# Seven of twelve weave distances changed in a two-layer gated trunk on one TensorE-bound core

## The chip, the core and the metric

The kernel runs on one core of a Trainium2 chip. The metric is the device time of one execution in microseconds. Before the change it was 1135.04 us, the median of three runs that lay between 1132.31 and 1135.21 us.

## What is computed

Two layers over a residual stream x of 512 positions by 1024 features, float32. Each layer normalises, scales and shifts x by a conditioning vector, makes one wide projection, runs three causal token mixers beside each other and merges them through gates.

```python
u = rms_norm(x, norm_g) * (1 + scale[:, None]) + shift[:, None]
z = u @ w_in     # aq ak av ag iq ik iw | bq bk bv bg | cq ck cv cg | ma mb mc
# A: indexer scores -> the 128 best keys of each query -> softmax attention, 8 heads, rotary
# B: sliding window of 128, 8 query heads on 2 key heads, learned sinks, rotary
# C: stick-breaking attention, 8 heads, strictly causal
merged = (sigmoid(ma) * (ya @ w_br_a) + sigmoid(mb) * (yb @ w_br_b) + sigmoid(mc) * (yc @ w_br_c))
return x + gate[:, None] * (merged @ w_out)      # ya, yb, yc already times silu(ag), silu(bg), silu(cg)
```

## The kernel before, in words

Everything is held transposed: features on the 128 partitions, the 512 positions along the free axis. A float32 product is made of three matmuls of a rounded type: the weight chunk is split into a high part `whi` and a low part `wlo`, the activation into `uh` and `ul` (or the two halves of `Y` for a mixer's output), and the products high-high, high-low and low-high are added. One column tile of the projection (`ttile`, 128 columns, for example aq2 or mb1) is two halves of 12 matmuls, and one output tile of a branch (`branch_item`, for example tile 1 of branch b) is 12 matmuls; such a group of 12 is called a block here. Each block needs one weight chunk of 128x512 that SyncE's queue (SP) loads into `wstage` and that VectorE, ScalarE or GpSimd split.

A mixer handles two heads at a time, four pairs p = 0 to 3, in three stages. Its score stage (`c_qk`, `softmax_qk`) multiplies `Q` by `KH` into five PSUM banks of the pool `ps_s` (four for B), adds the low products (`klow`), then VectorE adds the mask and takes the maximum (for A the mask is `score`, which must first have been through the top-k loop), ScalarE makes the exponentials and their sum, and VectorE or ScalarE scale them into the tile `X`. Its transpose stage (`softmax_tr32`) transposes `X` on VectorE in four pieces and moves 16 blocks of it by DMA into `U` (pairs 0 and 2) or into a part of `V5` (`V_675` in the order's rows; pairs 1 and 3); ScalarE's queue and SP share these issues. Its value stage (`value_run`, in `pairs`) multiplies `U` or `V` by the values on TensorE. Pair a0's value product rides along with the score stage of a1 (`RIDE`); a1 and a2 have theirs together, behind all of branch b; a3 has its own.

The order of the work comes about in two steps. First a weave (`Weave.run`) writes one list from seven streams: the three mixers, the indexer, the top-k loop, the conditioning products of this and the next layer, and the stream of projection and branch tiles. A stream that yields `wait(n)` is left out until n nanoseconds of planned TensorE work have been written. The distances are in the table `SPACE`: for mixer a, `a0` stands before a pair's score stage, `a1` between its scores and its transposes, `a2` between these and its value product; b and c likewise; `ag` and `as` space the conditioning products of this and the next layer, `t` the top-k steps.

```python
            yield need(f"ak{p}" if b == "a" else f"bq{p}")
            yield wait(SPACE[b + "0"])
            ...
            yield softmax_qk(b, p)
            ...
            yield wait(SPACE[b + "1"])
            yield softmax_tr(b, p)
            yield put(f"{b}free{p}")
            yield wait(SPACE[b + "2"])
```

Second, a recorder (`Recorder`) takes this list, gives buffers out in its order, and plans every instruction onto the engines by costs of its own and by how late each may go; it may move instructions past each other, and it chooses between VectorE, ScalarE and GpSimd for splits and copies. The programs of the five engines are then fixed: at run time each engine goes through its own list in order. All instructions come from two lines, L621 and, for `pairs`, L619.

Of the kernel before, what the change touches and what calls it, by code (L numbers as in the profile page):

```python
# [39 lines left out]
TOPK = 128  # L40
WARM = 8
BIG = 2.0 ** 100
SPACE = {"c0": 865, "c1": 7720, "c2": 1802, "a0": 1361, "a1": 13022, "a2": 500, "b0": 2448, "b1": 10119, "b2": 1676, "ag": 12129, "as": 6930, "t": 2422}
QCOST = 2408
BKEY = "cfree2"
LOAD_AHEAD, SPLIT_AHEAD = 4, 3
# [585 lines left out]
def op(cost, fn, *chunks):  # L632
    return ("op", cost, fn, [c + (phase[0],) for c in chunks])


def wait(ns):
    return ("wait", ns)


def need(e):  # L640
    return ("need", e)


def put(e):
    return ("set", e)
# [3 lines left out]
def trunk(ctx, tc, xT, vecs, w_ss, w_gt, w_first, w_t, w_v, w_br, w_o, rope, consts, out):  # L649
# [498 lines left out]
    def topk():  # L1148
        yield need("idx")
        for i in (1, 2, 3):  # L1150
            for n in range(TOPK // 8):
# [5 lines left out]
                yield op(0, fn)  # L1157
                yield wait(SPACE["t"])

# [81 lines left out]
    def mixer_c():  # L1241
        for p in range(4):
            yield need(f"ck{p}")
            yield wait(SPACE["c0"])
            yield from riders("c", p, RIDE.get(("c", p), ()), "in")
            yield c_qk(p)
            yield from riders("c", p, RIDE.get(("c", p), ()), "out")
            yield wait(SPACE["c1"])
            yield softmax_tr("c", p)
            yield put(f"cfree{p}")  # L1250
            yield wait(SPACE["c2"])
            for g in GROUPS["c"]:
# [131 lines left out]
    def softmax_tr(b, p):  # L1384
        if p in TR32.get(b, ()):
            return softmax_tr32(b, p)

        def fn():
            pt = st.pop(("p", p))
            pos, tpos = (bpos, btpos) if b == "b" else (apos, cpos)  # L1390
            nb = 4 if b == "b" else 5
            tb, PT, left = [None] * nb, [None] * nb, [0] * nb
            for e in range(2):
                for j in range(4):
                    left[tpos(e, j)[0]] += 1
            for e in range(2):
                for j in range(4):
                    bk, c0 = tpos(e, j)
                    if tb[bk] is None:
                        tb[bk] = sbank()  # L1400
                    for i in (range(j, min(4, j + 2)) if b == "b" else range(j, 4)):
                        sbk, s0 = pos(e, i)
                        kc = s0 + 128 * j - keys(b, i)[0]
                        PE.transpose(tb[bk][:, c0 + 128 * (i - j):c0 + 128 * (i - j) + 128], pt[sbk][:, kc:kc + 128], ident)
                    left[bk] -= 1
                    if not left[bk]:
                        W = 384 if b == "b" and bk >= 2 else 512
                        if all(v is None for v in PT):
                            whole = st["V5"] if b != "c" and p % 2 else rec.tile("U", [P, 5 * S], F32)
                        PT[bk] = whole[:, S * bk:S * bk + S]  # L1410
                        cast(PT[bk][:, :W], tb[bk][:, :W])
            st["pt", p] = PT
        return op(1520 if b == "b" else 2180, fn)
# [33 lines left out]
    def riders(b, p, ps, stage):  # L1447
        for q in ps:
            if stage == "out":
                yield put(f"{b}pv{q}")  # L1450
                continue
            yield need(f"{b}g{q}")
            if q and b != "c":
                yield need("brc" if b == "b" else "brb")

    def mixer_ab(b):
# [3 lines left out]
        for p in range(4):  # L1460
            yield need(f"ak{p}" if b == "a" else f"bq{p}")
            yield wait(SPACE[b + "0"])
            yield from riders(b, p, RIDE.get((b, p), ()), "in")
            yield softmax_qk(b, p)
            yield from riders(b, p, RIDE.get((b, p), ()), "out")
            yield wait(SPACE[b + "1"])
            yield softmax_tr(b, p)
# [348 lines left out]
```

## Time and profile before

| what | value |
|---|---|
| runs, us | 1132.31, 1135.04, 1135.21 |
| profiled execution, us | 1133.6 |
| its span from the first to the last instruction, us | 1131.7 |
| TensorE matmul busy | 1113.8 us, 98% |
| VectorE, ScalarE, GpSimd busy | 921.6, 607.0, 237.5 us |
| granted TensorE clock, mean | 0.999 |
| HBM read, written | 125.39 MB, 4.19 MB |

The names in the profile are those of the program without buffer numbers: `m<-zs` is the shift by half a head that the rotary step needs (its tile is m2), `U<-X` and `V<-X` are the DMAs of the transpose stage. An engine's row shows in brackets how long it stood idle before and what ended that. A matmul of 512 columns shows 0.39 us in its row, but the next one starts about 0.23 us after it; so TensorE can lose time between two starts without an idle time being shown.

### The profile page before, as it was taken

To read this page: it belongs to the slowest core of one execution; us is meant where nothing else is said; L and a number is where in the kernel's file an instruction comes from. 1 tells how busy PE (TensorE), PEld (TensorE's weight loads), DVE (VectorE), ACT (ScalarE), POOL (GpSimd) and SP (SyncE) were. 2 spreads that over 40 slices of the span, in tenths; PEclk is the share of its full clock that TensorE was granted. 3 is DMA by queue.
4 is the path that set the end of the run, shared out by engine and by line. 5 is a ranking of instruction groups with operands and counts; after the bars stand their busy time and mean duration, and the time that the engine had idled before them with its cause. 6 is when DMAs were issued, how large, how long until landed. Compare 5 with 4: busy or idle time off the path is not lost.

```text
span 1131.7 us, 17615 instructions
## 1 busy us (share of the span) xinstructions
PE 1113.8 (98%) x5539; PEld 922.8 (82%) x5539; DVE 921.6 (81%) x2016; ACT 607.0 (54%) x1285; POOL 237.5 (21%) x307
## 2 busy tenths in 40 slices
PE   8999999999999899999999999999999999999997
PEld 6899877788887687788898987777888788877886
DVE  8855999999999897787585479999999898666654
ACT  6744767663555553444355357685546366443343
POOL 1200344512223211010001004452212232111101
PEclk9999999999999999999999999999999999999999
DMA  9744343555465575455533443435635445525343
GB/s 358 233 122 123 98 118 105 147 163 146 116 182 159 148 213 160 140 149 180 179 114 103 110 131 85 132 102 163 182 103 144 135 141 151 150 82 149 94 131 102
DMA packets 95837, 162.48 MB, mean 144 GB/s; under 512 B 15104, under 2 KB 29696, under 8 KB 95744
## 3 DMA queue, kind: packets, MB, share of 16 engines
q1 hardware_dynamic: 86720, 147.44, 44.4%
q10 hardware_dynamic: 9024, 13.92, 4.3%
q8 instruction: 44, 0.72, 0.3%
q14 instruction: 49, 0.40, 0.1%
HBM read 125.39 MB, written 4.19 MB: 115 GB/s over the span
## 4 chain that ended last, share of the span: by engine, by line
PE 77%; DVE 15%; DMA 4%; SPq 1%; ACT 1%; issue 1%; POOL 0%; DVEq 0%; ACTq 0%; POOLq 0%
PE ps_z L621 60%; PE ps_s L621 14%; DVE t L621 4%; PE ps_s L619 2%; DVE X L621 1%; SPq L621 1%; DVE wlo L621 1%; DMA m<-zs 1%; PE ps_z L619 1%; DVE score L621 1%; DVE m L621 1%; DMA U<-X 1%; DVE zc L621 1%; DVE e L621 1%; DMA Y<-in_w_ss 1%
## 5 line engine op out<-in xcount | busy, mean ns | idle before, releaser
L621 PE MATMUL ps_z<-uh,whi 128*128 128x512 f32 (+1 forms) x905 | 352.9, 391 | 0.4 <-DVE G L621 0.3
L621 PE MATMUL ps_z<-ul,whi 128*128 128x512 f32 (+1 forms) x905 | 352.0, 390 | 0.2 <-DVE ul L621 0.2
L621 PE MATMUL ps_z<-uh,wlo 128*128 128x512 f32 (+1 forms) x905 | 350.3, 388 | 0.0
L621 DVE TENSOR_TENSOR wlo<-wstage,whi 128x512 fp32r<-128x512 f32 (+2 forms) x294 | 193.2, 661 | 99.2 <-ACT whi L621 90.0
L621 ACT CAST whi<-wstage 128x512 fp32r<-128x512 f32 (+2 forms) x226 | 133.7, 593 | 234.2 <-PE ps_z L621 176.2
L621 PEld LDWEIGHTS ps_z<-uh,whi 128*128 128x128 f32 x905 | 169.7, 188 | 36.7 <-issue 1.2
L621 PEld LDWEIGHTS ps_z<-ul,whi 128*128 128x128 f32 x905 | 169.9, 188 | 34.2 <-issue 1.2
L621 PEld LDWEIGHTS ps_z<-uh,wlo 128*128 128x128 f32 x905 | 169.9, 188 | 34.1
L621 POOL TENSOR_TENSOR wlo<-wstage,whi 128x512 fp32r<-128x512 f32 (+2 forms) x78 | 99.7, 1279 | 230.5 <-DVE whi L621 116.5
L621 PE MATMUL ps_z<-Y,whi 128*128 128x512 f32 x384 | 119.2, 391 | 0.2
L621 POOL CAST whi<-wstage 128x512 fp32r<-128x512 f32 (+1 forms) x72 | 43.6, 606 | 318.4 <-PE ps_z L621 177.6
L621 PEld LDWEIGHTS ps_z<-Y,whi 128*128 128x128 f32 x384 | 71.8, 188 | 16.7 <-DVE Y L621 1.1
L621 ACT ACTIVATE e<-e 128x512 f32<-128x512 f32 x96 | 59.9, 629 | 39.3 <-DVE e L621 30.9
L621 ACT ACTIVATE t<-t,nm 128x256 f32<-128x256 f32 (+3 forms) x128 | 65.2, 511 | 24.2 <-DVE nm L621 15.4
L621 PE MATMUL ps_z<-Y,wlo 128*128 128x512 f32 x192 | 74.4, 389 | 0.0
L621 ACT ACTIVATE t<-t 128x512 f32<-128x512 f32 x100 | 56.1, 627 | 0.3
L621 DVE STREAM_TRANSPOSE X<-X 128x640 f32<-128x640 f32 (+1 forms) x80 | 55.9, 738 | 0.4 <-ACT X L621 0.2
L621 DVE MAX8 m<-score 128x8 f32<-128x256 f32 (+2 forms) x96 | 53.4, 556 | 1.3
L621 ACT ACTIVATE e<-ps_z 128x512 f32<-128x512 f32 x68 | 40.3, 593 | 22.1 <-DVE wlo L621 5.2
L621 DVE MATCH_REPLACE8 score<-m,score 128x256 f32<-128x256 f32 (+2 forms) x96 | 52.0, 542 | 0.0
L621 PE MATMUL ps_s<-KH,Q 128*128 128x256 f32 (+3 forms) x280 | 49.7, 305 | 1.3 <-DVE e L621 0.7
L621 PEld LDWEIGHTS ps_s<-KH,Q 128*128 128x128 f32 x280 | 42.0, 189 | 8.8 <-DVE e L621 1.6
(211 smaller groups left out, 1953.5 us busy)
## 6 DMA issues: line engine op xcount, KB each, us to landing
wstage<-in_w_t SPq DMA_DIRECT2D x212, 256.0 KB, 2.7
wstage<-in_w_v SPq DMA_DIRECT2D x48, 182.0 KB, 2.3
m<-zs SPq DMA_DIRECT2D x128, 64.0 KB, 2.0
wstage<-in_w_gt SPq DMA_DIRECT2D x32, 256.0 KB, 2.7
wstage<-in_w_ss SPq DMA_DIRECT2D x32, 256.0 KB, 2.9
wstage<-in_w_o SPq DMA_DIRECT2D x32, 256.0 KB, 2.7
Y<-in_w_ss SPq DMA_DIRECT2D x15, 512.0 KB, 5.9
U<-X SPq DMA_DIRECT2D x65, 80.0 KB, 2.7
```

The lines of the kernel that those rows point to most:

```text
L619: self.real[engine].matmul(*[real(a) for a in q[:3]], start=q[3], stop=True, skip_group_check=True)
L621: made = getattr(self.real[engine], y.op)(*[real(a) for a in y.args], **{k: real(v) for k, v in y.kw.items()})
```

## The change

The table gets new distances; nothing else differs.

```diff
-SPACE = {"c0": 865, "c1": 7720, "c2": 1802, "a0": 1361, "a1": 13022, "a2": 500, "b0": 2448, "b1": 10119, "b2": 1676, "ag": 12129, "as": 6930, "t": 2422}
+SPACE = {"c0": 1375, "c1": 7720, "c2": 1666, "a0": 1325, "a1": 18965, "a2": 500, "b0": 2568, "b1": 9198, "b2": 1676, "ag": 12129, "as": 6748, "t": 2422}
```

The programs have the same 5319 rows on TensorE before and after, of which some stand elsewhere. On the others a handful of splits and copies change engine: VectorE has 1841 rows before and 1837 after, ScalarE 1331 and 1340, GpSimd 312 and 307. On TensorE the order is the same up to the end of mixer c, apart from two matmuls of tile mc2 that now stand between the first and the second matmuls of branch c; it differs from b's last pair to a's last pair, and is the same again from there on. The same holds in layer 2.

**TensorE, layer 1, the scores of pair a2.** Rows `uh`/`ul` are blocks of the projection, `KH,Q` the scores, `klow,Q` their low products. Before, they stand in pieces between the matmuls of tiles mb1 and aq3:

```order
L621 MATMUL ps_z<-ul_253,whi 128x512
L621 MATMUL ps_s<-KH,Q 128x512 x2
L621 MATMUL ps_z<-uh_425,wlo 128x512
L621 MATMUL ps_s<-KH,Q 128x384
L621 MATMUL ps_s<-KH,Q 128x128
L621 MATMUL ps_z<-uh_472,whi 128x512
L621 MATMUL ps_z<-ul_494,whi 128x512
L621 MATMUL ps_z<-uh_472,wlo 128x512
L621 MATMUL ps_s<-KH,Q 128x384
L621 MATMUL ps_s<-KH,Q 128x128
L621 MATMUL ps_s<-KH,Q 128x256 x2
L619 MATMUL ps_s<-klow_80,Q 128x512 x2
```

After, they stand together between the two halves of aq3:

```order
L621 MATMUL ps_z<-uh_384,wlo 128x512
L621 MATMUL ps_s<-KH,Q 128x512 x2
L621 MATMUL ps_s<-KH,Q 128x384 x2
L621 MATMUL ps_s<-KH,Q 128x128 x2
L621 MATMUL ps_s<-KH,Q 128x256 x2
L621 MATMUL ps_s<-klow_80,Q 128x256
L619 MATMUL ps_s<-klow_80,Q 128x512 x2
L619 MATMUL ps_s<-klow_80,Q 128x384 x2
```

The same happens to the scores of a0, a1 and a3. With it the distances between them change. In layer 1 the order has, from the last score row of a0 to the first of a1, 4 blocks before and 10 after; from the last of the main group of a1 to the first of a2, 5 blocks and some matmuls before and 10 after; from the last of a2 to the value product of a1 and a2, 21 blocks before and 13 after. From the scores of b3 to the value product of b2 and b3 it is 8 blocks and one or two matmuls before, 8 blocks less one matmul after. Tiles mb1 to mb4 and outputs 1 to 3 of branch b, most of which stood behind a2, now fill the gaps, and tile mb0 has moved from before b3's scores to behind them.

**SP, layer 1, the DMAs of pair b3's transposes.** Before, ten of the 16 stand on SP, and all four shifts of aq1 and then of ak1 behind them:

```order
L621 DMA V_675<-X 32x448 x10
L621 DMA wstage<-in_w_t 128x512
L621 DMA m_3838<-zs 32x512 x4
L621 DMA wstage<-in_w_ss 128x512
L621 DMA wstage<-in_w_t 128x512 x2
L621 DMA m_3892<-zs 32x512 x4
```

After, eight stand there (and eight on ScalarE's queue, which had six), and the shifts are mixed with more weight loads:

```order
L621 DMA V_675<-X 32x448 x8
L621 DMA wstage<-in_w_br_b 128x512
L621 DMA m_3806<-zs 32x512
L621 DMA wstage<-in_w_ss 128x512
L621 DMA m_3806<-zs 32x512 x2
L621 DMA wstage<-in_w_t 128x512
L621 DMA m_3806<-zs 32x512
L621 DMA wstage<-in_w_t 128x512
L621 DMA wstage<-in_w_br_b 128x512
L621 DMA wstage<-in_w_ss 128x512
L621 DMA m_3898<-zs 32x512 x4
```

**VectorE, layer 1, ahead of the masks of a0.** `ISA t,mx<-ps_s,score` is the instruction that adds a mask and takes the maximum. Before, the product with ak1's shift (m_3892) stands ahead of it, with six more rows between:

```order
L621 TENSOR_TENSOR e<-ps_s,G 128x512 x2
L621 TENSOR_TENSOR m_3892<-m_3892,rt 128x512
L621 TENSOR_TENSOR Y<-e,Y 128x512 x2
L621 TENSOR_TENSOR zc<-zc,m_3892 128x512
L621 TENSOR_SCALAR e<-e 128x512
L621 TENSOR_TENSOR wlo<-wstage,whi 128x512
L621 TENSOR_TENSOR Q<-zc,Q 64x512
L621 ISA t,mx<-ps_s,score_1242 128x512
```

After, it is aq1's shift (m_3806), an older one, that stands ahead, and ak1's is left to GpSimd:

```order
L621 TENSOR_TENSOR e<-ps_s,G 128x512 x2
L621 TENSOR_SCALAR score_1242<-score_1242 128x512
L621 TENSOR_TENSOR Y<-e,Y 128x512 x2
L621 CAST whi<-wstage 128x512
L621 TENSOR_SCALAR e<-e 128x512
L621 TENSOR_TENSOR zc<-ps_z,rt 128x512
L621 TENSOR_TENSOR m_3806<-m_3806,rt 128x512
L621 TENSOR_TENSOR G<-ps_z,e 128x512
L621 TENSOR_TENSOR wlo<-wstage,whi 128x512
L621 SCALAR_TENSOR_TENSOR wstage,dot<-wstage,csr 128x512
L621 ISA t,mx<-ps_s,score_1225 128x384
```

The last step of the top-k loop (`score<-score`) now stands nine rows ahead of the first mask instead of fifteen.

In mixer c of both layers two top-k instructions (one MATCH_REPLACE, one MAX) that stood on VectorE ahead of the transposes of pair c3 now stand behind them.

## The prediction

> **What bounds the kernel now.** I read the page first, then the stretch that the change rearranges (from the last block ahead of b3 to the scores of a3) as a window in each layer, then TensorE's rows and waits in it, then the queues that feed those waits.
>
> ```profile
> PE 1113.8 (98%) x5539; PEld 922.8 (82%) x5539; DVE 921.6 (81%) x2016; ACT 607.0 (54%) x1285; POOL 237.5 (21%) x307
> ...
> PE 77%; DVE 15%; DMA 4%; SPq 1%; ACT 1%; issue 1%; POOL 0%; DVEq 0%; ACTq 0%; POOLq 0%
> ```
>
> TensorE is busy for 98% of the span and holds 77% of the chain that ended last. Its work does not change, so the change can only move the little time that TensorE loses between its matmuls. How much that is in the rearranged stretch, the two windows show (window, its length, TensorE busy, weight loads, VectorE, ScalarE, GpSimd, granted clock, DMA):
>
> ```profile
> 298.44:455.75 157.31, 153.94 (x738) 122.83 (x736) 139.75 (x327) 80.85 (x180) 34.23 (x35) 1.00 0.59 169
> 853.53:1007.81 154.28, 153.21 (x738) 123.09 (x736) 125.92 (x279) 79.52 (x178) 33.02 (x34) 1.00 0.49 140
> ```
>
> The same 738 matmuls take 157.31 us in layer 1 and 154.28 us in layer 2 at the full clock: layer 1 loses at least 3.03 us. VectorE works 139.75 us of layer 1's window, so it is close behind TensorE but not the bound. The chain has the pace of undisturbed blocks:
>
> ```profile
> 940.98 57.33 PE ps_z L621 x252
> ```
>
> 57.33 / 252 = 0.2275 us from start to start, so a block of 12 is 2.73 us. Against this pace TensorE's rows show where it waits. Layer 1:
>
> ```profile
> 341.92 0.39 PE L621 MATMUL ps_z<-uh,whi 128*128 128x512 f32 x1
> 342.39 0.51 PE L621 MATMUL ps_s<-KH,Q 128*128 128x384 f32 x2
> ...
> 349.90 0.39 PE L621 MATMUL ps_z<-Y,wlo 128*128 128x512 f32 x1
> 350.63 0.50 PE L621 MATMUL ps_z<-uh,whi 128*128 128x512 f32 x1 [0.34 <-DVE G L621]
> ...
> 369.95 0.85 PE L619 MATMUL ps_s<-klow,Q 64*128 64x512 f32 x7
> 373.31 2.38 PE L619 MATMUL ps_z<-U,va 128*64 128x512 f32 x16 [2.51 <-DMA m<-zs]
> ...
> 377.79 0.39 PE L621 MATMUL ps_z<-ul,whi 128*128 128x512 f32 x1
> 378.32 0.72 PE L621 MATMUL ps_s<-KH,Q 128*128 128x512 f32 x2
> ...
> 380.96 0.85 PE L619 MATMUL ps_s<-klow,Q 64*128 64x512 f32 x7 [0.18 <-POOL klow L621]
> ...
> 413.57 0.39 PE L621 MATMUL ps_z<-Y,wlo 128*128 128x512 f32 x1
> 414.07 0.50 PE L621 MATMUL ps_z<-uh,whi 128*128 128x512 f32 x1
> ```
>
> Start to start less 0.23: 0.24 us at 341.92, 0.50 at 349.90, 0.30 at 377.79, 0.27 at 413.57; as idle time 2.51 at 373.31 and 0.18 at 380.96. That is 4.0 us. Layer 2:
>
> ```profile
> 887.63 0.39 PE L621 MATMUL ps_z<-ul,whi 128*128 128x512 f32 x1
> 888.35 1.33 PE L621 MATMUL ps_s<-KH,Q 128*128 128x512 f32 x4 [0.33 <-POOL KH L621]
> ...
> 896.09 0.39 PE L621 MATMUL ps_z<-ul,whi 128*128 128x512 f32 x1
> 897.13 0.50 PE L621 MATMUL ps_s<-KH,Q 128*128 128x384 f32 x2 [0.65 <-DVE e L621]
> ```
>
> 0.49 + 0.81 = 1.3 us. The Trainium skill (Trainium Kernel Development and Optimization, Performance Expectations) says that matmul busy time is a bad measure of how close a kernel is to its limit, because matmuls are pipelined. By busy time the two windows would have 3.37 + 1.07 = 4.4 us to give; the starts show 5.3 in waits alone, and the trace sides with the page.
>
> **Where the large wait comes from.** The value product of a0 rides behind a1's scores and needs all of `U`:
>
> ```profile
> 343.54 0.84 PE L619 MATMUL ps_s<-klow,Q 64*128 64x512 f32 x7
> ...
> 344.61 0.69 DVE L621 TENSOR_TENSOR m<-m,rt 128x512 f32<-128x512 f32 x1 [1.68 <-DMA m<-zs]
> ...
> 348.79 0.69 DVE L621 CUSTOM_DVE_ANT_0 t<-ps_s,score 128x512 f32<-128x512 f32 x1
> ...
> 361.94 3.02 DVE L621 STREAM_TRANSPOSE X<-X 128x640 f32<-128x640 f32 x4
> ...
> 362.81 8.54 ACTq L621 DMA_DIRECT2D U<-X  x9
> ...
> 362.86 6.82 SPq L621 DMA_DIRECT2D U<-X  x7
> ...
> DMA to landing us min/median/max: 2.1/2.5/4.9
> ```
>
> VectorE stands 1.68 us at ak1's shift and reaches a0's first mask at 348.79, though a0's scores are full at about 344.4, when the low products of the first row end. From the mask to the first transpose it takes 13.2 us, and ScalarE's nine issues end at 371.35; with 2.1 us of landing that is the 373.3 at which TensorE goes on. The bracket names another DMA of the same queue; the rows of `U` say that it is this one.
>
> **The change part by part.**
>
> *a0 to a1, layer 1.* The value product of a0 is due now when a1's low products end, at 369.95 + 0.85 = 370.8, 26.4 us behind a0's scores; it will be due after 10 blocks (27.3) and the scores of a1 (1.2 us for eight matmuls of 2560 columns in all at the pace above, and 0.85 for the low products), 29.3 us. What it needs took 373.3 - 344.4 = 28.9 us with the late start. Even with the same delay there is 0.4 us left; and the order takes ak1's shift out of VectorE's path ahead of the mask, so I expect the chain at about 25 us (28.9 less the 4.4 from 344.4 to 348.79). The 2.51 goes. Behind it nothing of a0 is late next.
>
> *The masks and banks.* The 0.24 at 341.92, the 0.30 and 0.18 at a2's scores and, in layer 2, 0.49 and 0.81 are TensorE entering scores for which a bank (`e` reads the banks of b's value product), `KH` or `klow` is late. After the change each pair's scores stand 10 blocks behind the keys' tile or behind the last user of the banks, except a0's, which stand two to two and a half blocks (5.5 to 6.8 us) behind b's value product. I take all of these as gone except half of layer 2's 0.81.
>
> *The breaks.* Scores in pieces also cost the changes between shapes. Layer 1 has five more breaks than layer 2: (3.03 - 2.7) / 5 = 0.07 us each. Eight go in layer 1 and three in layer 2: 0.8 us.
>
> *c3.* Two top-k rows move behind its transposes:
>
> ```profile
> 208.50 0.41 DVE L621 MATCH_REPLACE8 score<-m,score 128x256 f32<-128x256 f32 x1
> 208.82 0.55 DVE L621 MAX8 m<-score 128x8 f32<-128x384 f32 x1
> ...
> 218.22 0.39 PE L621 MATMUL ps_z<-Y,wlo 128*128 128x512 f32 x1
> 219.10 2.38 PE L619 MATMUL ps_s<-U,V 128*64 128x512 f32 x16 [0.49 <-DMA wstage<-in_w_gt]
> ...
> PE ps_s L619 <- DMA U<-X: 0.2, 1, 0.2
> ```
>
> They give up to 0.96 us to a wait of 0.49 in layer 1 and 0.2 in layer 2 (last row): 0.7 us. The two matmuls of mc2 that move I set at nothing; they last 0.45 us in each layer and can hide no more than that.
>
> *What moves on the queues.* Each pair's 16 block DMAs move with its transposes; their count is the same, SP issues eight of b3's instead of ten, and the weight loads for mb1 to mb4 move past them. The rows above give 8.54 / 9 = 0.95 and 6.82 / 7 = 0.97 us for each while the transposes run, so two fewer on SP free up to 2 us there and hold ScalarE as long. No wait of TensorE on `wlo` or `whi` shows in the stretch, so I cost the moved loads at nothing; their cover is the four chunks that lie ready, and if it is gone a late chunk costs its delay in full.
>
> *New waits.* The trace cannot show them. Their bounds are 0 and the 5.3 us that the old order loses now in the same stretch, for that order too was planned on the recorder's costs. I take 1.3, what layer 2 loses now, since the new distances are wide for a0 and a1 as layer 2's are.
>
> Sum: 4.0 + 1.3 - 0.4 + 0.8 + 0.7 = 6.4 us gained, less 1.3 new: 5.1 us. The profiled execution took 1133.6 us (span 1131.7), so 1128.5; the median of the runs is 1.4 above it, so I forecast 1129.9 us.
>
> **The rivals.**
>
> *B: a wait comes back elsewhere, and the time stays.* The nearest place is b's last value product in layer 1:
>
> ```profile
> 313.87 0.44 PE L621 MATMUL ps_z<-uh,whi 128*128 128x512 f32 x1
> ...
> 336.79 1.73 PE L619 MATMUL ps_s<-U,V 128*64 128x256 f32 x16
> 338.36 0.39 PE L619 MATMUL ps_s<-V 128*64 128x256 f32 x2
> ...
> L621 SPq DMA_DIRECT2D V<-X x10: 513/584/787, 328.5 to 334.4; - x10
> ```
>
> It begins 22.9 us behind b3's scores and needs `V` 1.5 us later; the last DMA is issued at 334.4 and, with the 2.0 us that a landing of this size takes at the median, is there at 336.4, 2.0 us early. The change makes the distance 8 blocks less a matmul, 21.6 us, so 0.7 us are left, plus what the split of eight and eight saves. Should VectorE run later there, TensorE loses up to its lag of 4.4 us seen at a0. With 3 to 5 us lost in such places the gain is 1 to 3 us: about 1133.
>
> *C: slower, by the value product of a1 and a2.* It now has 21 blocks behind a2's scores; it will have 13, 35.5 us.
>
> ```profile
> 388.31 0.40 PE L621 MATMUL ps_z<-uh,whi 128*128 128x512 f32 x1
> ...
> 419.93 0.51 SPq L621 DMA_DIRECT2D U<-X  x1
> ...
> 446.93 2.27 PE L619 MATMUL ps_s<-V,va 128*64 128x512 f32 x14
> ```
>
> Now a2's last block is issued 31.6 us behind its scores and lands up to 4.9 us later, at 36.5: that would be 1.0 us too late already. Against it: `X` is one buffer, and a2 had to wait for a1, whose scores stood five blocks ahead; with ten between them that goes, and a0's 25 us is the nearer figure. The gain of the forecast is used up when both layers lose 2.6 us there, a chain of 38.1 us, and at 39.8 us the time is 0.3% up: about 1138.5.
>
> The Trainium skill (TensorE: Matmul & The Clock Gate, Part 1) says that an idle window of about 3.4 us halves TensorE's clock until it has been busy as long again. By it C, with waits over 3.4 us, would be some 1.7 us dearer in each layer. No run here shows so long a wait; the one of 2.51 us left the clock of its window at 1.00:
>
> ```profile
> 360.00:375.00 15.00, 12.49 (x62) 9.53 (x62) 12.10 (x25) 4.47 (x9) 1.29 (x1) 1.00 0.73 197
> ```
>
> *D: nothing changes*, because the planner evens out the list. The order speaks against it: the scores stand elsewhere in both layers.
>
> **How the numbers follow.** A change of this kernel under about 0.3%, 3.4 us, can hardly be told from none. The forecast (a gain of 3.4 to 8) has 0.67; B and D 0.22, C 0.11. The range runs from the sum with no new wait and the other c3 and break terms in full, against the profiled execution's own time and a little below, 1126.0, up to B with 5 us lost, 1134.5; that leaves C and a small rest outside. Faster by over 0.3% is below 1131.6: 0.67; same 0.22; slower 0.11.
>
> **What would show it.** Right: TensorE's rows around a1's scores have no wait before the rows of `U`, and both windows come to 152.5 to 153.5 us. Wrong: brackets over 1 us at the value products of b2 and b3, or of a1 and a2, or `wlo` named as what TensorE waits for. I would be most wrong if VectorE, freed at a0, stood in a new place at a shift that lands late, since all behind it on that engine stands too.

## The result

The changed kernel takes 1127.82 us at the median of six runs (1127.05 to 1128.77); the kernel before took 1133.16 us in six runs on the same chip. The ratio is 0.995 with a 95% interval of 0.9937 to 0.9963: 5.3 us, or 0.5%, faster. The forecast was 1129.9 us with a range of 1126.0 to 1134.5. The profiled execution took 1127.05 us with a span of 1125.2 (1131.7 before). On its page TensorE's busy time is 4 us less than before (1113.8), and TensorE holds more of the chain that ended last:

```profile
PE 1109.6 (99%) x5539; PEld 923.2 (82%) x5539; DVE 922.4 (82%) x2012; ACT 608.7 (54%) x1294; POOL 228.8 (20%) x302
...
PE 86%; DVE 10%; DMA 2%; issue 1%; ACT 1%; SPq 0%; ACTq 0%; DVEq 0%
```

The two stretches from b3's to a3's scores, as windows of the kernel after (the columns are those of the prediction):

```profile
297.84:450.62 152.78, 152.59 (x737) 123.10 (x735) 140.38 (x327) 82.90 (x187) 37.79 (x38) 1.00 0.60 176
849.06:1001.34 152.28, 152.28 (x737) 123.17 (x735) 128.06 (x279) 80.27 (x182) 32.22 (x35) 1.00 0.50 142
```

Layer 1 came down from 157.31 to 152.78 us, layer 2 from 154.28 to 152.28: 6.5 us, all of the gain and more. The work between the two stretches became 0.65 us longer (397.78 to 398.43), what lies ahead of the first 0.6 shorter, most of it within the first 60 us of the program, where repeated executions differ by more than that (the first stretch begins at 297.84, 298.64 and 298.72 us in three executions of the kernel after); what lies behind the second is the same to 0.01 us. These parts are those of two single executions, which differ by 6.5 us in all, and not by the 5.3 of the medians. Around a0 and a1 in layer 1 TensorE's rows now read, without a bracket:

```profile
342.70 0.86 PE L619 MATMUL ps_s<-klow,Q 64*128 64x512 f32 x7
...
372.78 0.86 PE L619 MATMUL ps_s<-klow,Q 64*128 64x512 f32 x7
373.57 2.38 PE L619 MATMUL ps_z<-U,va 128*64 128x512 f32 x16
```

The loss between the stretches is in mixer c: TensorE's matmuls come 1.0 us later from c3's value product on, and 0.4 us come back in the 17 us behind it. c3's value product waits longer than before in both layers (0.49 and 0.2 us before):

```profile
PE ps_s L619 <- DMA U<-X: 2.2, 2, 1.6
```

This line of TensorE's waits sums both (total, times, longest); the rows of the two products:

```profile
218.44 2.38 PE L619 MATMUL ps_s<-U,V 128*64 128x512 f32 x16 [0.66 <-DMA U<-X]
...
770.04 2.37 PE L619 MATMUL ps_s<-U,V 128*64 128x512 f32 x16 [1.57 <-DMA U<-X]
```

SP's queue ahead of this wait in layer 2, first of the kernel before, then of the kernel after (start, time of the issues, what is issued):

```profile
763.12 2.41 SPq L621 DMA_DIRECT2D m<-zs  x4
766.28 5.55 SPq L621 DMA_DIRECT2D U<-X  x8
```

```profile
757.69 2.41 SPq L621 DMA_DIRECT2D m<-zs  x4
760.20 0.53 SPq L621 DMA_DIRECT2D wstage<-in_w_t  x1
760.84 6.61 SPq L621 DMA_DIRECT2D U<-X  x8
```

After, a load of a 256 KB weight chunk stands between the shifts and the blocks of `U`. Issue and landing of the 16 blocks, taken from the trace's DMA records (both queues in order of issue, us):

```
load of wstage   760.20 -> 763.76
block  1 to 4    760.55 -> 764.18   760.84 -> 764.50   761.28 -> 764.87   761.39 -> 765.41
block  5 to 8    762.00 -> 765.66   762.09 -> 765.98   762.73 -> 766.21   763.83 -> 766.65
block  9 to 12   764.20 -> 766.88   764.51 -> 767.21   764.89 -> 767.43   765.43 -> 767.61
block 13 to 16   765.68 -> 767.86   765.99 -> 768.22   766.24 -> 768.55   766.94 -> 769.95
```

Two things are to be seen. The first block lands 3.6 us after its issue, behind the load; before it was 2.0 us (766.25 to 768.25). And from the ninth to the fifteenth a block is issued 0.01 to 0.03 us after the block eight places earlier has landed (764.18 and 764.20, 764.50 and 764.51, 765.41 and 765.43). It is the programs that wait: their lists give the landings eight counters in turn, and a DMA is issued when the one before it on its counter is there. In none of the traces of this case do the two queues have more than eight of their 944 DMAs under way, and none is issued before its predecessor on the same counter has landed. So whatever lands late at the head holds back the issues behind it.

### The profile page after: what moved, and what is told of

The parts are those of the page before. It is cut to its first block, busy times and chain, and to the rows that moved or that the text cites. A ratio compares the mean times of both kernels' runs of the same rounds, so it can differ in the third digit from the quotient of the medians.

```text
span 1125.2 us, 17626 instructions
## 1 busy us (share of the span) xinstructions
PE 1109.6 (99%) x5539; PEld 923.2 (82%) x5539; DVE 922.4 (82%) x2012; ACT 608.7 (54%) x1294; POOL 228.8 (20%) x302
## 4 chain that ended last, share of the span: by engine, by line
PE 86%; DVE 10%; DMA 2%; issue 1%; ACT 1%; SPq 0%; ACTq 0%; DVEq 0%
PE ps_z L621 67%; PE ps_s L621 15%; DVE t L621 4%; PE ps_s L619 3%; DMA U<-X 2%; DVE wlo L621 1%; PE ps_z L619 1%; DVE e L621 1%; DMA Y<-in_w_ss 1%; DVE X L621 1%; DVE score L621 1%; DVE ps_s L621 1%; DVE wstage L621 0%; DVE m L621 0%; DVE klow L621 0%
## 5 line engine op out<-in xcount | busy, mean ns | idle before, releaser
L621 DVE TENSOR_TENSOR wlo<-wstage,whi 128x512 fp32r<-128x512 f32 (+2 forms) x312 | 207.8, 670 | 89.3 <-ACT whi L621 78.0
L621 ACT CAST whi<-wstage 128x512 fp32r<-128x512 f32 (+2 forms) x237 | 140.0, 593 | 222.2 <-PE ps_z L621 155.0
L621 POOL CAST whi<-wstage 128x512 fp32r<-128x512 f32 (+1 forms) x76 | 46.6, 614 | 388.3 <-PE ps_z L621 216.5
L621 POOL TENSOR_TENSOR wlo<-wstage,whi 128x512 fp32r<-128x512 f32 (+2 forms) x60 | 76.4, 1274 | 156.1 <-DVE whi L621 75.1
L621 DVE MAX8 m<-score 128x8 f32<-128x384 f32 (+2 forms) x96 | 53.3, 557 | 1.4
L621 DVE SCALAR_TENSOR_TENSOR wstage<-wstage,csr 128x512 f32<-128x512 f32 x64 | 44.9, 705 | 7.4 <-DMA wstage<-in_w_ss 6.9
L621 PE MATMUL ps_s<-KH,Q 128*128 128x256 f32 (+3 forms) x280 | 47.4, 303 | 0.0
```

What stands on the lines that cost most here:

```text
L621: made = getattr(self.real[engine], y.op)(*[real(a) for a in y.args], **{k: real(v) for k, v in y.kw.items()})
```

## The experiments

All lengths of stretches below run between the same matmuls as the windows above, except for the longer a1, whose order these windows do not fit. "Between" is the work from the end of the stretch in layer 1 to the start of that in layer 2.

| kernel | ratio to before, 95% interval | layer 1 | between | layer 2 |
|---|---|---|---|---|
| before | 1 | 157.31 | 397.78 | 154.28 |
| after | 0.995 (0.9937 to 0.9963) | 152.78 | 398.43 | 152.29 |
| a1 alone new | 0.998 (0.9969 to 0.9991) | 156.91 | 398.03 | 153.15 |
| after, a1 as before | 0.9968 (0.9956 to 0.998) | 154.34 | 398.26 | 152.51 |
| after, a1 longer still | 1.0069 (1.005 to 1.0088) | - | - | - |
| after, c3's load behind its blocks | 0.9949 (0.9937 to 0.996) | 153.51 | 397.74 | 152.29 |
| the same, and its split | 0.9938 (0.9924 to 0.9952) | 154.41 | 396.90 | 152.29 |
| the same in layer 2 alone | 0.9936 (0.9924 to 0.9948) | 153.75 | 397.07 | 152.29 |
| after, beside the second | 0.9938 (0.9926 to 0.9951) | 152.57 | 398.53 | 152.29 |
| after, beside the third | 0.9946 (0.9934 to 0.9958) | 152.48 | 397.95 | 152.29 |
| before, a0's loads behind its blocks | 1.0024 (1.0015 to 1.0033) | 160.89 | 397.77 | 154.15 |
| the same, splits later | 1.0001 (0.9992 to 1.001) | 157.11 | 397.77 | 154.57 |
| before, ak1's shift later | 1.0006 (0.9996 to 1.0015) | 157.34 | 397.79 | 154.48 |

### Which of the distances: a1 alone

Four of the seven new numbers need no run: with c0, c2, a0 or b0 put back, alone or all together, the lists of all five engines are row for row those of the kernel after. What is left is a1, b1 and `as`. With `as` alone put back TensorE's list stays the same and some rows of the other engines move; it has no run of its own.

```diff
-"a1": 13022
+"a1": 18965
```

> The kernel before with only the distance a1 new (18965); the others as before. Theory: the gain has two parts, a1 (a0's value product rides with a1's scores, which come later) and b1 (a0's scores no longer start inside the value product of b2 and b3). With a1 alone a1's scores stand 73 rows of the list behind a0's in layer 1 instead of 46 (109 with all distances new), so the wait of 2.51 us ahead of a0's value product goes, but a0's scores stay in two pieces and the small waits around them stay: about 1131 us, 2 to 3 us faster than before. Rival 1, a1 carries everything: 1128. Rival 2, b1 carries everything: 1133, no gain. In mixer c a load of a weight chunk now stands directly ahead of c3's blocks on SyncE's queue, so c3's value product in layer 2 should wait 1 to 1.6 us as in the kernel after; if it waits 0.3 or less, the load is not the cause.

1131.67 us, ratio 0.998: 2.3 us faster, the size that was expected. In its profile a0's value product no longer waits, but layer 1 gains only 0.4 us, since a new wait stands at a0's own first scores, which in this order come directly behind ak0's key:

```profile
335.52 0.73 PE L621 MATMUL ps_s<-KH,Q 128*128 128x512 f32 x3 [1.93 <-ACT KH L621]
```

It costs more than 1.93 us. From 337.20 on seven matmuls take 0.43 us from start to start instead of 0.23, 1.4 us in all, and the windows of this run show the granted clock (last column but two) at half:

```profile
325.00:333.00 8.00, 8.00 (x37) 6.60 (x37) 7.87 (x19) 3.48 (x7) 1.29 (x1) 1.00 0.61 173
...
337.20:340.00 2.80, 2.80 (x8) 2.23 (x7) 2.25 (x8) 0.00 (x0) 0.33 (x1) 0.50 0.52 159
```

c3's value product waited 0.9 us at the most, less than the 1 to 1.6 expected, with another load ahead of its blocks.

### The other distances without a1

```diff
-"a1": 18965
+"a1": 13022
```

> The kernel after with a1 back at 13022; the other six distances new. a0's scores then stand whole, and a1's 89 rows behind them (8 blocks). The value product of a0 is due about 24.4 us behind its scores (8 blocks of 2.73 us, 1.2 and 0.85 us of a1's scores, 0.5 of the low products), and the blocks of U took 27.5 us in layer 1 and 24.2 us in layer 2 of the kernel after. Theory: TensorE waits about 3 us for U in layer 1 and under 0.5 in layer 2; 1130 to 1132 us, slower than the kernel after by 2 to 4 us. Rival: the new place of a0's scores is what shortens the chain, it comes to under 24.4 us here, and the time is that of the kernel after, 1127 to 1128.

1130.58 us, ratio 0.9968: 3.6 us faster than before and about 2 us behind the kernel after, as expected. The wait for `U` in layer 1 is there, but it is 1.1 us and not 3:

```profile
PE ps_z L619 <- DMA U<-X: 1.1, 1, 1.1
```

Without a1, b1 (with `as`) brings 3.0 of layer 1's 4.5 us and 1.8 of layer 2's 2.0; a1 brings the rest on top of it, but alone it brings 0.4 and 1.1. So b1 (with `as`) is the larger half of the change, and the two are not additive. In its order a0's scores stand in one piece behind b's value product; that this is what brings the time was not separated from the other rows that it moves. This execution also has a wait of 0.6 us for ScalarE's `e` at 359.10 us.

### a1 longer still

```diff
-"a1": 18965
+"a1": 24500
```

> The kernel after with the distance a1 at 24500 instead of 18965. In the list of layer 1 a1's scores then stand 141 rows behind a0's instead of 109, but a2's and a3's scores are in pieces again and a3's second piece stands close ahead of a3's value product. a0's value product had 2.4 us to spare in layer 1 of the kernel after, so it gains nothing there. Theory (the distance has an upper side, where the chains of a2 and a3 lack the room that a0's got): TensorE waits 1 us or more at a2's or a3's value product or scores in each layer, 1130 to 1134 us. Rival: longer is as good, since the chains of a1 and a2 had 8.7 us to spare; 1127 to 1129 us.

1140.51 us, ratio 1.0069: slower than before by 6 us, more than the theory's range. TensorE's order differs from that of the kernel after up to behind a3's value product. From the start of the stretch (297.84 us in the kernel after, 298.08 here) to the first matmul from which the two orders are the same again (480.50 and 485.51) the profiled execution loses 4.8 us in layer 1; in layer 2 (from 849.06 to 1031.21, and from 853.86 to 1041.72) it loses 5.7. Each other part is the same to 0.3 us. The two largest waits stand behind a3's scores, one ahead of an output tile in layer 1 and one ahead of a3's value product in layer 2:

```profile
477.61 0.73 PE L621 MATMUL ps_z<-Y,whi 128*128 128x512 f32 x2 [2.55 <-ACT e L621]
...
1033.66 2.61 PE L619 MATMUL ps_s<-V,va 128*64 128x512 f32 x6 [3.67 <-DMA wstage<-in_w_t]
```

The windows behind them have the granted clock at 1.00 and at 0.54, so the second costs some more than its 3.67 us:

```profile
477.60:481.00 3.40, 3.39 (x15) 1.86 (x17) 1.12 (x3) 0.63 (x1) 0.00 (x0) 1.00 0.69 205
1033.60:1037.00 3.40, 3.34 (x12) 1.38 (x14) 0.00 (x0) 0.14 (x1) 0.00 (x0) 0.54 0.02 8
```

### c3's wait: the load behind its blocks

In both layers one row of SP's list of the kernel after moves; all other lists stay as they are.

```diff
 DMA m_8295<-zs 32x512 x4
-DMA wstage<-in_w_t 128x512
 DMA U<-X 32x640 x8
+DMA wstage<-in_w_t 128x512
```

> The kernel after with one row of SyncE's queue moved in each layer: the load of a weight chunk that stands directly ahead of c3's eight blocks of U goes behind them, where the kernel before has it; the rows of the four other engines are the same. Theory: the load holds back the landing of the blocks issued right behind it (first landing 3.6 us after its issue, against 2.0 in the kernel before), and since each DMA of the two queues is issued only when the one eight places earlier has landed, all 16 are late; without it the last block lands 1 to 1.6 us earlier and TensorE's waits at c3's value product (1.57 us in layer 2, about 0.6 to 0.8 in layer 1) go to 0.3 or less: 1.2 to 2 us faster than the kernel after, about 1126. Rival 1: VectorE's transposes set the landing, not the load; the waits stay and the time is that of the kernel after. Rival 2: the moved chunk comes late to its own split and TensorE waits for it: no faster than the kernel after, with a wait on wlo or whi in the trace.

The cause is shown, the gain is not. In layer 2 the first block lands 2.07 us after its issue (762.34 to 764.41) instead of 3.6, the 16 blocks take 7.7 us from the first issue to the last landing instead of 9.4, and the product waits for nothing. The time, 1128.43 us, is that of the kernel after: a wait of 0.79 us stands 5 us behind, where the three executions of the kernel after have 0.36 us once and no bracket twice.

```profile
770.19 2.37 PE L619 MATMUL ps_s<-U,V 128*64 128x512 f32 x16
...
775.38 0.72 PE L621 MATMUL ps_z<-Y,whi 128*128 128x512 f32 x2 [0.79 <-POOL Y L621]
```

GpSimd and VectorE of the same run say why (the moved load lands at 771.04):

```profile
771.19 0.61 POOL L621 CAST whi<-wstage 128x512 fp32r<-128x512 f32 x1 [5.24 <-DVE Q L621]
```

```profile
771.84 0.69 DVE L621 TENSOR_TENSOR wlo<-wstage,whi 128x512 fp32r<-128x512 f32 x1 [0.68 <-POOL whi L621]
```

VectorE stands 0.68 us for the split of the moved chunk, and c3's gating, of which TensorE needs `Y`, is queued behind it. In layer 1 the wait did not go (0.79 us from start to start, 0.83 after): there the first block lands 2.1 us after its issue, but the last six take 3.2 to 3.5 us. Three loads now follow the blocks at once, but the first of these six was issued 2.2 us ahead of the first load (214.56 and 216.79 us), so it stays open what makes them late.

### The load and its split

```diff
-TENSOR_TENSOR wlo<-wstage,whi 128x512
 ...
 TENSOR_TENSOR e<-ps_s,G 128x512
 ...
 TENSOR_TENSOR Y<-e,Y 128x512
+TENSOR_TENSOR wlo<-wstage,whi 128x512
```

> As the trial with the weight load behind c3's blocks, on the kernel after, and the low split of that load on VectorE also moved, from ahead of c3's gating (the e and Y that TensorE waited 0.8 us for there) to behind it, in both layers. Theory: the wait at c3's value product in layer 2 stays away (0.3 or less instead of 1.57) and the new wait of 0.8 us for Y goes: 1.3 to 2 us faster than the kernel after. Rival: Y still comes late because the value product itself ends later than the order wants, or wlo comes late for tile mc2: a wait of 0.5 us or more in the 10 us behind c3's value product, and at most 0.8 us faster than the kernel after.

> The kernel after, unchanged, beside the three others on one chip, so that they can be compared with it directly. Expected 1127 to 1129 us with the wait of 1.6 us at c3's value product in layer 2 in its trace again; if that wait is not there, it was a matter of one execution and not of the order.

Both waits in layer 2 are gone: "between" is 396.90 us against 398.53 in the kernel after on the same chip, 1.6 us less, as the theory has it. The wait at c3's value product in layer 2 is there in all three executions of the kernel after, with 1.57, 1.07 and 0.84 us. The time is the same all the same, 1127.58 and 1127.64 us: in the profiled execution layer 1's stretch is 1.8 us longer, most of it at two places where none of its rows was changed:

```profile
335.58 1.73 PE L619 MATMUL ps_s<-V 128*64 128x256 f32 x16 [0.67 <-DMA V<-X]
...
451.23 1.10 PE L621 MATMUL ps_s<-KH,Q 128*128 128x384 f32 x5 [0.36 <-DVE e L621]
```

### The same in layer 2 alone

The edit is the last two in layer 2, with layer 1's lists those of the kernel after.

> The kernel after with the load behind c3's blocks and its low split behind c3's gating in layer 2 alone; layer 1 keeps the rows of the kernel after. In the trial with both layers the stretch from b3's to a3's scores in layer 1 had got 1.8 us longer (V for b2 and b3's value product late by 0.7, a3's scores by 0.8), while the work between the two stretches had got 1.6 us shorter. Theory: the move pays in layer 2 and its cost in layer 1 comes from the move there; the work between the stretches is 396.8 to 397.2 us, the stretch of layer 1 stays at 152.5 to 152.9, and the time is 1.3 to 1.8 us under the kernel after. Rival: the longer stretch of layer 1 is what that stretch does by chance from run to run, and appears here too: the time is within 0.5 us of the kernel after.

> The kernel after, unchanged, beside the trial with layer 2 alone and the one with a longer distance, on the same chip: 1127 to 1128.5 us, the work between the stretches 398.3 to 398.6, the stretches 152.5 to 152.9 and 152.2 to 152.4.

1126.87 us against 1127.85 for the kernel after on the same chip; the intervals (0.9924 to 0.9948 and 0.9934 to 0.9958) overlap, so a version that beats the kernel after by 1 us is possible but not shown. "Between" is 397.07 us against 397.95 and 398.53. Layer 1's stretch is 153.75 us, 1.0 to 1.3 more than in the three executions of the kernel after, with unchanged rows; 0.9 us of it from start to start at a3's scores, where the bracket has 0.4:

```profile
PE ps_s L621 <- DVE e L621: 0.4, 1, 0.4
```

The rival is right in so far that this wait comes without any change in that layer. It was in all three executions with the load moved and in none of the three of the kernel after; whether that is chance stays open.

### a0's wait in the kernel before: the three loads ahead of its blocks

```diff
-DMA wstage<-in_w_t 128x512
-DMA wstage<-in_w_ss 128x512
-DMA wstage<-in_w_t 128x512
 DMA U<-X 32x640 x7
 DMA m_4196<-zs 32x512 x4
+DMA wstage<-in_w_t 128x512
+DMA wstage<-in_w_ss 128x512
+DMA wstage<-in_w_t 128x512
```

Some of their splits on VectorE and ScalarE move back too.

> The kernel before with the three weight loads that stand directly ahead of a0's blocks of U in layer 1 (issued at 360.71, 361.33 and 362.05 us) moved behind these blocks and the four shifts that follow, and their splits and the one product that reads them moved back on VectorE and ScalarE to fit; TensorE's row order is that of before. Theory: these loads hold back the first landings (4.4 us after the issue) and through the eight-places rule ScalarE's nine issues; without them ScalarE's issues take about 6 us instead of 8.5, the last block lands by 371, and the wait of 2.51 us ahead of a0's value product falls to 0 to 0.7: about 2 us faster than before, 1131. Rival, the reading of the prediction: the late start of the masks on VectorE sets it; the wait stays at 2 to 2.5 us and the time at 1133.

The blocks came as the theory says: ScalarE's nine issues take 5.91 us instead of 8.54 and a0's value product waits 0.12 us instead of 2.51 (the 0.7 that the expectation of the next trial names is the wait of an earlier product, at 171.76 us). But the kernel is 2.4 us slower (1136.58 us), since VectorE now stands for a moved load ahead of a product that TensorE needs, and TensorE's clock halves behind that wait:

```profile
364.75 5.91 ACTq L621 DMA_DIRECT2D U<-X  x9
```

```profile
375.46 0.43 DVE L621 CAST whi<-wstage 128x512 fp32r<-128x512 f32 x1 [2.24 <-DMA wstage<-in_w_t]
```

```profile
379.89 0.79 PE L621 MATMUL ps_z<-uh,whi 128*128 128x512 f32 x1 [2.58 <-DVE e L621]
```

```profile
379.80:383.00 3.20, 2.99 (x7) 1.99 (x8) 3.20 (x16) 1.94 (x4) 2.87 (x5) 0.50 0.05 17
383.00:386.00 3.00, 3.00 (x11) 2.48 (x12) 3.00 (x7) 1.53 (x5) 2.08 (x2) 0.50 0.21 53
```

With the splits placed later still, behind the `e` that TensorE waited for:

```diff
 TENSOR_TENSOR m_4196<-m_4196,rt 128x512
 TENSOR_TENSOR zc<-zc,m_4196 128x512
 TENSOR_TENSOR e<-ps_z,G 128x512
+CAST whi<-wstage 128x512
+TENSOR_TENSOR wlo<-wstage,whi 128x512
+SCALAR_TENSOR_TENSOR wstage,dot<-wstage,csr 128x512
 ...
 ISA t,mx<-ps_s,score 128x512
```

> As the first trial with the three weight loads behind a0's blocks, on the kernel before, but with the splits of these loads placed later: on VectorE behind ak2's shift and the e of b's first output, on ScalarE behind the copies of KH, so that neither engine stands waiting for a load ahead of work that TensorE needs. Theory: the waits of 2.58 us for e and the half clock after it go, what is left is the gain at a0's value product (wait 0.7 instead of 2.51): 1131.5 to 1132.5, about 2 us faster than before. Rival: the loads are needed where they stood, and another wait of 1 us or more appears in the 15 us behind them: 1134 or more.

Now the first block is issued when it was before (362.95 against 362.81 us), the nine issues take 5.89 us, and a0's value product starts at 371.22 with no idle time, 2.1 us earlier than before:

```profile
362.95 5.89 ACTq L621 DMA_DIRECT2D U<-X  x9
```

```profile
371.22 2.37 PE L619 MATMUL ps_z<-U,va 128*64 128x512 f32 x16
...
377.26 1.02 PE L621 MATMUL ps_s<-KH,Q 128*128 128x512 f32 x2 [1.15 <-ACT Y L621]
```

So without the loads ahead of the blocks that wait is gone. Yet the time is that of the kernel before (1134.32 us, ratio 1.0001): as the rival has it, another wait of more than 1 us follows. a2's first scores wait 1.15 us at 377.26, and a3's 0.6 us from start to start at 405.70. The bracket of the first names ScalarE's `Y`, and VectorE's first mask of a1, which frees the first bank, also ends just ahead of 377.26. On both engines rows of the moved loads stand right ahead:

```profile
376.12 0.62 ACT L621 CAST whi<-wstage 128x512 fp32r<-128x512 f32 x1 [0.64 <-DMA wstage<-in_w_t]
376.65 0.61 ACT L621 CAST Y<-e 128x512 fp32r<-128x512 f32 x1
```

```profile
374.25 0.42 DVE L621 CAST whi<-wstage 128x512 fp32r<-128x512 f32 x1
374.70 0.69 DVE L621 TENSOR_TENSOR wlo<-wstage,whi 128x512 fp32r<-128x512 f32 x1
375.31 0.68 DVE L621 SCALAR_TENSOR_TENSOR wstage<-wstage,csr 128x512 f32<-128x512 f32 x1
...
376.42 0.68 DVE L621 CUSTOM_DVE_ANT_0 t<-ps_s,score 128x512 f32<-128x512 f32 x1
```

VectorE spends 2.2 us, from 374.25 to 376.42, on the rows that the trial put there, and only then reaches the masks. So the trial shows that this cure gained nothing. It does not show that the old order would pass the time on by itself, since the new wait stands behind the trial's own rows.

### a0's late start on VectorE

```diff
-TENSOR_TENSOR m_3892<-m_3892,rt 128x512
 TENSOR_TENSOR Y<-e,Y 128x512 x2
 TENSOR_SCALAR e<-e 128x512
 TENSOR_TENSOR wlo<-wstage,whi 128x512
 TENSOR_TENSOR Q<-zc,Q 64x512
+TENSOR_TENSOR m_3892<-m_3892,rt 128x512
 TENSOR_TENSOR zc<-zc,m_3892 128x512
```

> The kernel before with the product of ak1's shift on VectorE (it waited 1.68 us for the shift in layer 1) and the sum behind it moved behind four rows that can go at once, directly ahead of a0's first mask; ScalarE's first copy of KH follows it. Theory of the prediction (the late start on VectorE sets the wait ahead of a0's value product): masks, transposes and the blocks of U all come about 1.5 us earlier, the wait falls from 2.51 to about 1.0, the time by 1.5 us to about 1132.5. Rival (the landing of the blocks behind the three weight loads sets it, and these loads move with the rest or not at all): the wait falls by less than 0.7 us and the time stays within 1 us of the kernel before.

1134.81 us, ratio 1.0006: no change. The trial did not do what it was meant to, since the first mask came only 0.26 us earlier (348.53 against 348.79), so it can't speak against the theory; the wait ahead of a0's value product was 1.9 us.

```profile
PE ps_z L619 <- DMA m<-zs: 1.9, 1, 1.9
```

```profile
347.19 0.69 DVE L621 TENSOR_TENSOR m<-m,rt 128x512 f32<-128x512 f32 x1
...
348.53 0.68 DVE L621 CUSTOM_DVE_ANT_0 t<-ps_s,score 128x512 f32<-128x512 f32 x1
```

## Why the prediction was right, and where it was not

- **The waits in the stretch (4.0 and 1.3 us, less 0.4, and 0.8 for the breaks: 5.7).** Right; the stretches gave 4.5 and 2.0 us, 6.5 together, and the windows, forecast at 152.5 to 153.5, are 152.78 and 152.28, the second a little under. The waits that the prediction added up are gone, but whether each is worth its own length was not shown: the trial that cured the 2.51 us alone won 0.2 us in the stretch, and it had put other work ahead of the next masks. That the new order removes the waits by putting ten blocks between the scores of one pair of a and the next is the likely reading; with eight between a0's and a1's, in the trial with a1 put back, most of the gain was there already. The breaks were not measured by themselves.
- **a0's chain.** The distance was right, the chain not. The product now starts 30.0 us behind a0's scores (343.56 to 373.57; forecast 29.3). The blocks took 27.4 us (the last lands at 370.96), not 25; with the old distance of 26.4 us the product would by this have waited an estimated 1.0.
- **The 0.95 us of an issue "while the transposes run".** Wrong cause. The issues are slow because the later ones wait for the landing of the one before on their counter, and those landings were held back by three loads; with the loads behind, the same nine issues take 0.65 us each (5.89 / 9). The late start on VectorE, named as the root of the 2.51 us, was not enough to make it: with the first issue at the same time and the loads away the wait was gone. Whether an earlier start alone would have cured it stays open, since the trial for it moved the first mask by only 0.26 us.
- **c3 (0.7 us gained).** The wrong sign. The waits went from 0.7 in all to 1.7 to 2.2 in the three executions of the kernel after, a loss of 1.0 to 1.5. I counted the two top-k rows that leave VectorE and left out the load that moved ahead of the blocks on SP, though the lists show it. With that load moved the wait in layer 2 went; what delays c3 in layer 1 stays open.
- **New waits (1.3 us lost).** None in the stretch, apart from 0.19 us that one of three executions of the kernel after shows (the kernel before has a like one of 0.34); the loss at c3 belongs to the term above.
- **The sum (5.1 us).** That it lies so near the 5.3 us of the medians was partly luck. c3's term was 1.7 to 2.2 us too high, the new waits took off 1.3 us that were not lost, and the stretches gave 0.8 us more than their terms; these errors nearly cancel. On two other chips the medians of before and after are 6.4 and 6.2 us apart. The forecast time lies 2.1 us above the measured one, mostly because the kernel before came to 1133.16 us in six runs and not to the 1135.04 that the forecast started from.
- **Rival B.** Its place is real: the 0.7 us that the prediction left b2 and b3's value product were used up in one execution of a trial (a wait of 0.67 for `V`), never in the kernel after.
- **Rival C.** Too dark. a2's blocks were issued up to 430.7 us and the product of a1 and a2 begins at 441.06 with a1's part; even with the longest landing of those on SP, 4.7 us, 5.7 are left, and the trace has the last one at 432.35. A chain that lacks room does show on the far side, though at a3 and not at a1 and a2: with a1 at 24500 a3's value product in layer 2 waits 3.67 us, and the kernel is 6 us slower than before.

```profile
404.69 0.86 PE L619 MATMUL ps_s<-klow,Q 64*128 64x512 f32 x7
...
428.24 2.42 SPq L621 DMA_DIRECT2D U<-X  x4
...
441.06 2.37 PE L619 MATMUL ps_s<-V,va 128*64 128x512 f32 x16
```

- **Rival D.** It fell: the time moved by more than 3.4 us.
- **What SP's moved loads cost in the stretch (nothing).** Right there: no wait for `wlo` or `whi` shows. The fault was to ask only for chunks that come late, and not for blocks that come late behind a chunk.

## What to carry to other kernels

When a list is rearranged, look at what now stands directly ahead of each group of small DMAs that the busiest engine waits for: here one load ahead of c3's blocks moved the first landing from 2.0 to 3.6 us, and with at most eight DMAs under way on the two queues the delay was handed on to the issues behind it. A load that is put elsewhere also needs a place for its splits: in three trials here they then stood ahead of something that TensorE needed, and the time that was won at one wait was lost again behind it. And a distance has two sides: with 10 blocks between a0's and a1's scores the waits went, with 13 the scores of a2 and a3 came in pieces again and larger waits stood behind a3's.

## What the hardware showed that was not expected

TensorE's granted clock halved after idle times shorter than the one that had left it alone. After 1.93 us it stood at 0.50 from 336.90 to 340.32 us (0.43 us from start to start instead of 0.23), around the end of 2.58 us at 0.50 from 379.25 to 386.08, and around the end of 3.67 us at 0.50 from 1033.30 to 1036.71, by the traces' clock records. It stayed at 1.00 after 2.51 us in the kernel before, after 2.55 us in the trial with the longest a1 and after 1.57 us in the kernel after. The Trainium skill (TensorE: Matmul & The Clock Gate, Part 1) has the clock fall after at least one idle window of about 3.4 us. The runs with 1.93 and 2.58 us differ from it, and there the measurement decides. The page also says that this window runs freely, which would let the same idle time be punished in one place and not in another; no run here tests that. The records would fit it: the times at half are 3.4, 6.8 and 3.4 us long, and they begin 1.4 us behind the end of the idle time in the first case and 0.6 and 0.4 us ahead of it in the others. For a sum like the prediction's it means that a new wait of 1.93 us cost 3.3 us (1.93 and the 1.4 behind it).

A landing is not a fixed time: a block of 80 KB landed 2.0 us after its issue with nothing large ahead, 3.6 us behind one load of 256 KB, and 4.5 us behind three (362.81 to 367.26 in the kernel before). Within one burst of 16 such blocks with no load among them it grew from 2.0 to 3.3 us (the second trial on a0's loads, issued from 362.95 to 368.12).
